# SBUF laid out by tile size: 2 KB tiles first, weight tiles 2304 bytes apart, half-width weights 64 bytes into their tile

## The chip, the core and the metric

The kernel runs on one core of a Trainium2 chip. The metric is the device time of one execution in microseconds, here as the median of three runs. SBUF is the on-chip memory of 128 partitions; an address below is a byte address within each partition.

## What is computed

The reference is two transformer blocks with two layers each, over 512 positions of width 1024, in float32. Cut to what matters here:

```python
# block 1, layer:  x += .5*rmsnorm(swiglu(rmsnorm(x)));  x += rmsnorm(token_mixer(rmsnorm(x)));  x += .5*rmsnorm(swiglu(...))
# block 2, layer:  x = layer_norm(ALPHA*x + mixer2(x));  x = layer_norm(ALPHA*x + swiglu(x))
def swiglu(h, w_gate, w_up, w_down):            # w_gate, w_up: 1024 x 2816, w_down: 2816 x 1024
    return (jax.nn.silu(h @ w_gate) * (h @ w_up)) @ w_down
proj = h @ w_in                                 # the mixers: projections, attention variants, then
return mixed @ w_out                            # an output projection
```

Nearly all the work is `activation @ weight` with weights that are read from DRAM once.

## The kernel before

**Number format.** Every float32 product runs as three products in the format float32r: a value is split in a high part and the rest, and `hi*hi + hi*lo + lo*hi` is summed in PSUM. Activations are split once and stay in SBUF: `h` (input of a projection, 16 tiles), `gu` (the gated activations of an FFN, 44 tiles) and `m` (the mixed heads, in the same 44 places), each tile 128 x 512 values, 2048 bytes in a partition.

**Weights.** `weights` loads 1024 columns of weights into a `raw` tile (3 places) by DMA on SyncE, and for each 512 columns writes a pair of `ws` tiles (14 places of 2048 bytes): ScalarE or VectorE copies the high part, VectorE or ScalarE subtracts it for the rest. A pair of `ws` tiles feeds 12 matmuls of 128 weight columns each.

**Matmuls.** `project` computes 128 output features. Its weight operand is 128 x 128 of a `ws` tile and its moving operand the activations, over all 512 positions (512 columns) or, for the first units and the last units of a stage, over one half of them (256 columns, the range `r`), so that a half can be normalised while the other is being multiplied. `vproj` computes the value projections the other way round: the `h` tile is the weight operand and a `ws` tile moves, 256 columns wide (280 for the last). Each matmul has its own weight load, and in the records the load for one matmul runs beside the matmul before it.

**Order.** A recorder collects all operations, a list scheduler with fixed costs sets the order of each engine, and `issue` emits them. A tile name has a list of places ("slots"); the scheduler gives each buffer a slot, and the pool allocates a slot's SBUF the first time that `issue` meets one of its buffers. So before the change the addresses follow the order of first use:

| operand | places | start address modulo 128 bytes |
|---|---|---|
| `ws` | 14 | all 64 |
| `h` | 16 | 64 in 12 places, 96 in 2, 0 in 2 |
| `gu`, `m` | 44 | 0 in 40 places, 64 in 4 |
| `raw` | 3 | all 64 |

A 128-column piece of a `ws` tile begins a multiple of 512 bytes into it, and the second half of an activation tile 1024 bytes into it, so these numbers hold for the operands as they are used. Below, the **phase** of a matmul is the address of the next matmul's weights (the load that runs beside it) less that of its own moving tile, modulo 128: 0 is called the same phase, 64 the opposite phase. In the program before, counting neighbouring matmuls of one shape, `h` with 256 columns has the same phase in 2542 pairs of 3386 and with 512 columns in 4446 of 5963; `gu` with 256 columns has the opposite phase in 2825 of 3111 and with 512 columns in 1432 of 1574.

## Time and profile before

| what | value |
|---|---|
| median of three runs | 3496.48 us (3493.1 to 3496.89) |
| profiled execution | 3497.46 us, span 3495.7 us |
| TensorE matmul busy | 3428.8 us, 98% of the span |
| VectorE, ScalarE busy | 2225.2 us (64%), 1738.7 us (50%) |
| granted TensorE clock, mean | 0.994 of full speed |
| bytes moved by DMA | 393.32 MB, mean 113 GB/s |

The span is the time from the first to the last instruction of the profiled execution, and 1.8 us of its own time lie around it. A recorded matmul lasts some 280 ns with 256 columns and some 397 ns with 512, but starts of neighbours are much closer than that, since they are pipelined. The quantity to look at is therefore the distance from one start to the next: the length of an unbroken row of the timeline less the last matmul's own length, divided by the count less one.

### The profile page before, as it was taken

To read this page: it belongs to the slowest core of one execution; us is meant where nothing else is said; L and a number is where in the kernel's file an instruction comes from. 1 tells how busy PE (TensorE), PEld (TensorE's weight loads), DVE (VectorE), ACT (ScalarE), POOL (GpSimd) and SP (SyncE) were. 2 spreads that over 40 slices of the span, in tenths; PEclk is the share of its full clock that TensorE was granted. 3 is DMA by queue.
4 is the path that set the end of the run, shared out by engine and by line. 5 is a ranking of instruction groups with operands and counts; after the bars stand their busy time and mean duration, and the time that the engine had idled before them with its cause. 6 is when DMAs were issued, how large, how long until landed. Compare 5 with 4: busy or idle time off the path is not lost.

```text
span 3495.7 us, 54570 instructions
## 1 busy us (share of the span) xinstructions
PE 3428.8 (98%) x20340; PEld 2964.8 (85%) x20340; DVE 2225.2 (64%) x5360; ACT 1738.7 (50%) x3681; POOL 26.8 (1%) x74
## 2 busy tenths in 40 slices
PE   8999999999999999999999999999999999999998
PEld 7887988888898889888888898879888988798888
DVE  7443898854467445998844376888333878883336
ACT  6333577643354333676533355666332656763324
POOL 0000000000000000000000000000000000000000
PEclk9999999999999999999999999999999999999999
DMA  5224532332354224522422363115223531143234
GB/s 188 97 90 139 181 103 70 127 127 96 91 163 136 94 92 139 165 65 90 137 93 95 105 194 100 50 41 173 92 97 100 188 106 61 40 141 113 93 93 135
DMA packets 121755, 393.32 MB, mean 113 GB/s; under 512 B 14829, under 2 KB 19990, under 8 KB 121489
## 3 DMA queue, kind: packets, MB, share of 16 engines
q1 hardware_dynamic: 121488, 389.83, 34.9%
q8 instruction: 160, 2.62, 0.3%
q14 instruction: 107, 0.87, 0.1%
HBM read 385.01 MB, written 4.77 MB: 112 GB/s over the span
## 4 chain that ended last, share of the span: by engine, by line
PE 84%; DVE 11%; ACT 3%; DMA 1%; issue 1%; SPq 0%; ACTq 0%; DVEq 0%
PE mm L681 76%; PE at L681 3%; DVE hw L681 2%; PE ah L681 2%; DVE ws L681 2%; PE pv L678 2%; DVE tc L681 1%; PE nb L681 1%; DVE sm L681 1%; DVE row L681 1%; DVE x L681 1%; DVE h L681 1%; DMA raw<-in_wg_dram 0%; ACT ws L681 0%; DMA cw<-in_cw_dram 0%
## 5 line engine op out<-in xcount | busy, mean ns | idle before, releaser
L681 PE MATMUL mm<-h,ws 128*128 128x512 f32 (+1 forms) x9792 | 2041.4, 358 | 13.0 <-DVE ws L681 9.7
L681 PEld LDWEIGHTS mm<-h,ws 128*128 128x128 f32 x9792 | 1623.7, 189 | 286.2 <-DVE ws L681 13.5
L681 ACT ACTIVATE ws<-raw 128x512 fp32r<-128x512 f32 (+1 forms) x1368 | 828.3, 615 | 1299.8 <-PE mm L681 1248.9
L681 DVE TENSOR_TENSOR ws<-raw,ws 128x512 fp32r<-128x512 f32 (+1 forms) x1432 | 952.6, 671 | 805.0 <-ACT ws L681 701.9
L681 PE MATMUL mm<-gu,ws 128*128 128x256 f32 (+1 forms) x4752 | 776.0, 318 | 0.0
L681 PEld LDWEIGHTS mm<-gu,ws 128*128 128x128 f32 x4752 | 674.6, 188 | 75.7 <-issue 4.4
L681 PE MATMUL mm<-ws,h 128*128 128x256 f32 (+1 forms) x1344 | 239.8, 294 | 4.3 <-ACT ws L681 1.3
L681 DVE TENSOR_TENSOR te<-te,mm 128x256 f32<-128x256 f32 (+1 forms) x228 | 99.0, 459 | 209.3 <-PE mm L681 209.3
L681 PEld LDWEIGHTS mm<-ws,h 128*128 128x128 f32 x1344 | 196.6, 190 | 9.6 <-issue 2.2
L681 PE MATMUL mm<-m,ws 128*128 128x256 f32 (+1 forms) x1248 | 203.1, 310 | 0.6 <-DVE Q L681 0.6
L681 PEld LDWEIGHTS mm<-m,ws 128*128 128x128 f32 x1248 | 167.1, 188 | 12.1 <-DVE Q L681 1.0
L681 ACT ACTIVATE row<-row,sm 128x384 f32<-128x384 f32 (+2 forms) x265 | 146.1, 564 | 39.3 <-DVE sm L681 38.1
L681 ACT ACTIVATE gu<-te 128x256 fp32r<-128x256 f32 (+1 forms) x224 | 95.4, 452 | 113.6 <-DVE te L681 113.5
L681 DVE TENSOR_TENSOR gu<-te,gu 128x256 fp32r<-128x256 f32 (+1 forms) x228 | 105.4, 464 | 14.4 <-ACT gu L681 3.0
L681 DVE TENSOR_TENSOR te<-mm,rt 128x256 f32<-128x256 f32 x176 | 67.7, 418 | 65.2 <-PE mm L681 65.2
L681 PE MATMUL at<-c_ident,row 128*128 128x128 f32 x528 | 100.5, 276 | 3.7 <-DVE row L681 1.9
L681 DVE CUSTOM_DVE_ANT_0 row<-at,T 128x128 f32<-128x128 f32 (+1 forms) x180 | 88.3, 507 | 6.3 <-PE at L681 4.9
L681 PE MATMUL ah<-hw 128*128 128x128 f32 (+1 forms) x512 | 87.8, 286 | 2.4 <-DVE hw L681 2.3
L681 ACT ACTIVATE te<-te 128x256 f32<-128x256 f32 x176 | 67.2, 417 | 45.2 <-DVE te L681 43.7
L681 ACT ACTIVATE hw<-hw 128x256 f32<-128x256 f32 (+1 forms) x176 | 74.7, 459 | 30.0 <-DVE hw L681 14.3
L681 PEld LDWEIGHTS ah<-hw 128*128 128x128 f32 x512 | 77.1, 192 | 9.4 <-DVE hw L681 2.7
L681 DVE TENSOR_TENSOR hw<-hw 128x256 f32<-128x256 f32 (+1 forms) x196 | 79.5, 422 | 5.0 <-ACT hw L681 4.3
(222 smaller groups left out, 2560.7 us busy)
## 6 DMA issues: line engine op xcount, KB each, us to landing
raw<-in_wg_dram SPq DMA_DIRECT2D x156, 512.0 KB, 3.3
raw<-in_wu_dram SPq DMA_DIRECT2D x156, 512.0 KB, 3.3
raw<-in_wd_dram SPq DMA_DIRECT2D x144, 512.0 KB, 3.5
raw<-in_wd_dram SPq DMA_DIRECT2D x72, 384.0 KB, 3.2
raw<-in_wout_dram SPq DMA_DIRECT2D x52, 512.0 KB, 3.3
raw<-in_w_f_dram SPq DMA_DIRECT2D x52, 512.0 KB, 3.3
raw<-in_win_f_dram SPq DMA_DIRECT2D x44, 512.0 KB, 3.4
raw<-in_win_v_dram SPq DMA_DIRECT2D x20, 512.0 KB, 3.6
```

Source lines behind the costliest of these rows:

```text
L678: r = nc.tensor.matmul(*args[i:i + 3], start=start and i < 6, stop=stop and i >= len(args) - 6, **kw)
L681: r = getattr(getattr(nc, op.eng), op.meth)(*args, **kw)
```

## The change

Before the first instruction is emitted, `issue` now allocates every SBUF slot in a fixed order: slots of 2048 bytes first, then `ws`, then the others from wide to narrow. A `ws` tile is declared with 576 columns (2304 bytes) instead of 512, and 512 of them are used: the first 512 where the matmuls that use the weights have 512 columns, and those from column 16 (64 bytes in) where they have 256 (`half`: `project` over half the positions, and `vproj` always).

```diff
+            first = {}
+            for op in order:
+                for b in op.bufs:
+                    if not b.dram and b.tag not in PSUM:
+                        first.setdefault(b.slot or id(b), b)
+            width = lambda b: size.get(b.slot, b.bytes())
+            for b in sorted(first.values(), key=lambda b: (width(b) != 2048, b.tag != "ws", -width(b), b.seq)):
+                real(b)
             for op in order:
                 for b in op.bufs:
                     real(b)
...
+WS_COLS = 576
...
-    def weights(self, src, n, w):
+    def weights(self, src, n, w, half):
         nc = self.nc
+        skip = 16 if half else 0
...
-            hi, lo = self.tile("ws", 512, F32R), self.tile("ws", 512, F32R)
+            hi, lo = (self.tile("ws", WS_COLS, F32R)[:, skip:skip + 512] for _ in range(2))
...
-            wt = self.weights(src[:, c * 128:(c + n) * 128], n, 128)
+            wt = self.weights(src[:, c * 128:(c + n) * 128], n, 128, r[1] - r[0] < S)
...
-            wt = self.weights(src[:, k0 * ncol:(k0 + n) * ncol], n, ncol)
+            wt = self.weights(src[:, k0 * ncol:(k0 + n) * ncol], n, ncol, True)
```

The instructions of each engine, their order and their waits are the same before and after; what differs is where the tiles lie. In the changed program every 2048-byte tile (`x`, `h`, `gu` and its sharers, `y`, `te`, `tc`) begins at 0 modulo 128, each 2048 bytes after the one before; the 14 `ws` tiles begin at 0 modulo 128, 2304 bytes apart; and weights for 256 columns begin at 64 modulo 128. By the definition above every matmul of `project` with 256 columns then has the opposite phase, every one with 512 columns the same phase, and every one of `vproj` (moving tile at 64, weights at 0) the opposite phase. The `raw` tiles begin at 0 modulo 128.

## Rows read from the trace of the kernel before

**Rows 1.** The page: busy time of each engine, granted clock by slice, chain's shares.
```profile
PE 3428.8 (98%) x20340; PEld 2964.8 (85%) x20340; DVE 2225.2 (64%) x5360; ACT 1738.7 (50%) x3681; POOL 26.8 (1%) x74
...
PEclk9999999999999999999999999999999999999999
...
PE 84%; DVE 11%; ACT 3%; DMA 1%; issue 1%; SPq 0%; ACTq 0%; DVEq 0%
PE mm L681 76%; PE at L681 3%; DVE hw L681 2%; PE ah L681 2%; DVE ws L681 2%; PE pv L678 2%; DVE tc L681 1%; PE nb L681 1%; DVE sm L681 1%; DVE row L681 1%; DVE x L681 1%; DVE h L681 1%; DMA raw<-in_wg_dram 0%; ACT ws L681 0%; DMA cw<-in_cw_dram 0%
```

**Rows 2.** Groups by shape: xcount, busy us, mean ns of one, idle before.
```profile
L681 PE MATMUL mm<-h,ws 128*128 128x512 f32 x6336 | 1585.3, 397 | 0.4 <-ACT VH L681 0.2
L681 DVE TENSOR_TENSOR ws<-raw,ws 128x512 fp32r<-128x512 f32 x1344 | 916.8, 687 | 743.8 <-ACT ws L681 669.1 <-PE mm L681 57.2 <-ACT tt L681 4.8
L681 ACT ACTIVATE ws<-raw 128x512 fp32r<-128x512 f32 x1283 | 794.6, 628 | 1205.1 <-PE mm L681 1154.6 <-DMA raw<-in_wg_dram 11.0 <-DMA raw<-in_wu_dram 6.3
L681 PE MATMUL mm<-h,ws 128*128 128x256 f32 x3456 | 474.1, 287 | 12.6 <-DVE ws L681 9.7 <-DVE te L681 1.5 <-DVE Q L681 0.7
L681 PE MATMUL mm<-gu,ws 128*128 128x256 f32 x3168 | 407.0, 280 | 0.0
L681 PE MATMUL mm<-gu,ws 128*128 128x512 f32 x1584 | 398.5, 396 | 0.0
L681 PE MATMUL mm<-ws,h 128*128 128x256 f32 x1152 | 206.3, 292 | 4.1 <-ACT ws L681 1.3 <-DVE ws L681 1.2 <-DVE sm L681 0.6
L681 PE MATMUL mm<-m,ws 128*128 128x256 f32 x960 | 131.2, 281 | 0.0
L681 PE MATMUL mm<-m,ws 128*128 128x512 f32 x288 | 93.0, 407 | 0.6 <-DVE Q L681 0.6
L681 PE MATMUL mm<-ws,h 128*128 128x280 f32 x192 | 33.5, 304 | 0.2 <-DVE NQ L681 0.2
```

**Rows 3.** Timeline of PE: start us, us, xcount; two stretches of 256 columns.
```profile
2092.57 4.09 PE L681 MATMUL mm<-h,ws 128*128 128x256 f32 x33
2086.89 3.95 PE L681 MATMUL mm<-h,ws 128*128 128x256 f32 x32
```

**Rows 4.** Timeline of PE: two other stretches of 256 columns.
```profile
1645.71 14.13 PE L681 MATMUL mm<-m,ws 128*128 128x256 f32 x123
3417.17 10.51 PE L681 MATMUL mm<-gu,ws 128*128 128x256 f32 x91
```

**Rows 5.** Timeline of PE: four stretches of 512 columns.
```profile
1877.70 4.51 PE L681 MATMUL mm<-h,ws 128*128 128x512 f32 x19
1888.77 4.54 PE L681 MATMUL mm<-h,ws 128*128 128x512 f32 x19
1911.00 4.53 PE L681 MATMUL mm<-h,ws 128*128 128x512 f32 x19
1939.83 21.78 PE L681 MATMUL mm<-gu,ws 128*128 128x512 f32 x93
```

**Rows 6.** Timeline of PE: whole stages of each kind, all phases that occur.
```profile
2790.23 15.53 PE L681 MATMUL mm<-h,ws 128*128 128x256 f32 x130
2407.51 30.69 PE L681 MATMUL mm<-h,ws 128*128 128x256 f32 x257
979.77 33.37 PE L681 MATMUL mm<-gu,ws 128*128 128x256 f32 x288
633.32 14.22 PE L681 MATMUL mm<-m,ws 128*128 128x256 f32 x122
2099.94 5.50 PE L681 MATMUL mm<-ws,h 128*128 128x256 f32 x45
2443.05 192.87 PE L681 MATMUL mm<-h,ws 128*128 128x512 f32 x835
1937.99 53.09 PE L681 MATMUL mm<-gu,ws 128*128 128x512 f32 x228
```

**Rows 7.** Windows: PE, PEld, DVE, ACT, POOL busy us, PEclk, DMA share, GB/s.
```profile
20.00:65.00 45.00, 45.00 (x364) 44.71 (x365) 40.34 (x99) 31.47 (x56) 0.00 (x0) 1.00 0.65 216
688.00:715.00 27.00, 27.00 (x228) 26.71 (x226) 25.41 (x56) 16.45 (x34) 0.00 (x0) 1.00 0.66 215
2407.00:2438.00 31.00, 31.00 (x264) 31.00 (x263) 25.68 (x56) 21.89 (x47) 0.00 (x0) 1.00 0.67 217
```

## Prediction

> **What bounds the kernel now.** I read the page first. TensorE's matmul row is busy 98% of the span, VectorE 64%, ScalarE 50%, and the chain that ended last is 84% TensorE, 76% of the span in matmuls into `mm` alone, the projections [rows 1]. The granted clock is above nine tenths in every slice, so the clock has nothing to give [rows 1]. A kernel in that state gets faster only by fewer matmuls or by a smaller distance from one matmul's start to the next. The change leaves every instruction in place, so the whole question is that distance.

> I therefore read the groups by shape for the counts [rows 2] and the timeline of TensorE for the distances, each an unbroken row's length less one matmul's own length (0.28 us with 256 columns, 0.39 us with 512), over the count less one. I chose stretches by the phase that the addresses give, with one or two odd pairs at most in each:

> - 256 columns, same phase (`h`): (4.09 - 0.28) / 32 = 119.1 ns and 3.67 / 31 = 118.4 ns [rows 3].
> - 256 columns, opposite phase (`m`, `gu`): (14.13 - 0.28) / 122 = 113.5 ns and 10.23 / 90 = 113.7 ns [rows 4].
> - 512 columns, same phase (`h`): (4.51 - 0.39) / 18 = 228.9, 230.6 and 230.0 ns, mean 229.8 [rows 5].
> - 512 columns, opposite phase (`gu`): (21.78 - 0.39) / 92 = 232.5 ns [rows 5].

> So the two widths want different things: with 256 columns the opposite phase is 5 ns shorter, with 512 columns the same phase is 2.7 ns shorter. Nothing in these rows waits for another engine. What the reader is to see is that the distance differs between equal instructions, with the address as the only known difference.

> [...]

> **The change, part by part.** Whole stages show what the mix of phases costs today [rows 6]: `h` with 256 columns (15.53 - 0.28) / 129 = 118.2 and 30.41 / 256 = 118.8, say 118.5 ns; `gu` with 256 columns 33.09 / 287 = 115.3 ns, `m` 13.94 / 121 = 115.2 ns; `vproj` 5.22 / 44 = 118.6 ns; `h` with 512 columns 192.48 / 834 = 230.8 ns; `gu` with 512 columns 52.70 / 227 = 232.2 ns. After the change all of the 256-column ones should stand at 113.6 ns and all of the 512-column ones at 229.8 ns. With the counts of [rows 2]:

> - `h`, 256 columns: 3456 x 4.9 ns = 16.9 us.
> - `gu` and `m`, 256 columns: 3168 x 1.7 + 960 x 1.6 = 6.9 us.
> - `vproj`: (1152 + 192) x 5.0 = 6.7 us.
> - `h`, 512 columns: 6336 x 1.0 = 6.3 us.
> - `gu` and `m`, 512 columns: (1584 + 288) x 2.4 = 4.5 us.

> Together 41.3 us, if every nanosecond counted. It doesn't, because part of these matmuls is not on the chain. All the `mm` matmuls at the distances above take about 2940 us (6336 x 230.8 + 1872 x 232.2 + 3456 x 118.5 + 4128 x 115.3 + 1344 x 118.6), and the chain holds 76% of 3495.7 = 2657 us of them: 0.9. I take 0.9 for the long, unbroken stages: all of 512 columns (10.8 us give 9.7) and the last units, `gu` and `m` with 256 (6.9 give 6.2).

> The first units of a stage, `h` with 256 columns, are worse off. There a pair of `ws` tiles lasts only 12 x 118.5 ns = 1.42 us, and in these stretches VectorE is busy 40.34 of 45 us, 25.41 of 27 and 25.68 of 31 [rows 7], 90, 94 and 83%; the first of them already runs at 45 us / 364 = 123.6 ns, above the 118.5 of an unhindered row, and the group has its idle time behind `ws` of VectorE, 9.7 us [rows 2]. If TensorE gets 4% faster, VectorE's 94% becomes 98%: it still fits, but hardly, and any wait for `ws` that TensorE now meets a little earlier takes the gain back. Nothing gained is one end, 0.9 the other; I take 0.6, nearer the upper end because the tile that limits (687 ns of VectorE in 1.42 us [rows 2]) leaves room: 10.2 us. DMA moves 216 GB/s there [rows 7] and would have to move 4% more; the group has no idle time from a DMA, so I cost it at nothing, and if it does not follow, the same 10.2 us are lost.

> For `vproj` the trace has almost no steady stretch in the opposite phase with the `ws` tile moving, so the price is bounded by 118.6 ns (nothing) and 113.6 ns (all). These matmuls sit between attention heads, with waits around them. I take 0.4: 2.7 us.

> What the change adds costs nothing that a row shows. A `ws` tile is 256 bytes longer, but the same 512 columns are written and read. The writers of `ws` and the readers of `raw` start at other addresses; the copy and the subtraction occur before at one phase only, so a loss there is not excluded. At 687 ns each and 1344 of them, 2% longer would add 18 us to VectorE, which is idle for 36% of the span and would show it only in the start stages, some 4 us. I take 0. A gain there would be as small.

> Sum: 9.7 + 6.2 + 10.2 + 2.7 = 28.8 us. The profiled execution took 3497.46 us in its own time (span 3495.7 and 1.8 around it), so the changed one should take 3468.7; the median of the runs is 1.0 us lower, which gives **3468 us**, 0.8% faster.

> **The rivals.**

> - **Only the 256-column part works.** The changed 512-column matmuls all read at 0 modulo 128 with weights at 0; the same phase before was 64 with 64. If the absolute address counts too, they could stand at the 232.5 ns of `gu` [rows 5]: 6336 x 1.7 x 0.9 = 9.7 us lost instead of 9.7 gained, and 3468 + 19 = 3487 us. For it: the three stretches of the same phase scatter from 228.9 to 230.6. Against: each of them lies below every opposite one. The same time, about 3490, results if the start stages and `vproj` give nothing because VectorE sets their pace.
> - **Slower.** With 512 columns all weights and all moving tiles now begin at one phase, for stretches of hundreds of matmuls instead of 18. If then each weight load costs what it costs in the same phase with 256 columns, 4.9 ns, the 8208 matmuls lose 8208 x 4.9 x 0.9 = 36 us against 19 gained: 3496.5 + 17 = 3514 us. The point from which this decides is a distance with 512 columns of about 231.1 + 19 / (8208 x 0.9) = 234 ns. Against it: no same-phase row comes near it.
> - **The change does nothing.** If `h` is slow for a reason other than its phase, such as its place in the start stages beside a busy VectorE, distances stay and the time is 3496 us within 0.2%. [...] For it: the slow and the fast rows of 256 columns do come from different stages. Against: `m` and `gu` at 113.6 ns come from stages with weight conversions at the same pace, 12 matmuls to a pair, and `h` with 512 columns, in a calm stage, is the faster one.

> **How the numbers follow.** The forecast has 0.59, the first rival with its variant 0.19, no effect 0.14, slower 0.08. About 0.2% (7 us) is what a measurement of this kernel can tell from no change; 3487 and 3490 lie 0.27% and 0.19% below the median, so a little of the first rival goes to "same". That gives faster 0.76, same 0.16, slower 0.08. The range: below, the 512 columns at their best row (228.9, another 0.9 x 8208 x 0.9 = 6.6 us), `h` at 0.9 (5.1 us) and `vproj` at 0.9 (3.3 us) give 3453, and with a distance a little under any seen 3446; above, the first rival's 3487 to 3490. The forecast's own range is 3453 to 3480.

> **What would show it.** In the changed kernel's timeline: rows of `h` with 256 columns at 113 to 115 ns instead of 118.5; `gu` with 256 columns near 113.6 throughout, without the rise at its four odd tiles; `h` and `gu` with 512 columns both at 229 to 231; `vproj` at 114 or still 118.6. In the windows of the start stages, VectorE's share should rise by some 4% of itself, and the waits of `mm` for `ws` on VectorE may grow from 9.7 us. The copy into `ws` on ScalarE should stay at 628 ns and the subtraction on VectorE at 687 [rows 2]. The prediction is wrong if 512 columns stand above 231, or if `h` with 256 columns stays at 118 while its addresses are in the opposite phase.

## Result and the profile after

The changed kernel takes 3456.68 us (median, 3453.73 to 3457.36) against 3495.95 us for the kernel before in the same comparison: a ratio of 0.9887, 95% interval 0.987 to 0.9905, or 39 us less. The forecast was 3468 us, 28 less. Its profiled execution took 3457.36 us in its own time with a span of 3455.6 us.

The page of the changed kernel, busy time of each engine, answers to [rows 1]:

```profile
PE 3386.9 (98%) x20340; PEld 2952.9 (85%) x20340; DVE 2222.5 (64%) x5360; ACT 1739.2 (50%) x3681; POOL 26.9 (1%) x74
...
PE 82%; DVE 12%; ACT 3%; issue 1%; DMA 1%; SPq 0%; ACTq 0%; DVEq 0%
```

TensorE's busy time falls by 41.9 us, the other engines' stays. The groups by shape of the changed kernel (count, busy us, mean ns of one, idle before) answer to [rows 2]:

```profile
L689 PE MATMUL mm<-h,ws 128*128 128x512 f32 x6336 | 1561.6, 393 | 0.5 <-DVE D L689 0.2 <-ACT VH L689 0.2
L689 DVE TENSOR_TENSOR ws<-raw,ws 128x512 fp32r<-128x512 f32 x1344 | 916.4, 687 | 721.5 <-ACT ws L689 654.5 <-PE mm L689 50.0 <-ACT tt L689 4.7
L689 ACT ACTIVATE ws<-raw 128x512 fp32r<-128x512 f32 x1283 | 794.7, 628 | 1166.7 <-PE mm L689 1111.1 <-DMA raw<-in_wg_dram 9.3 <-DMA raw<-in_wu_dram 5.8
L689 PE MATMUL mm<-h,ws 128*128 128x256 f32 x3456 | 466.8, 285 | 13.2 <-DVE ws L689 10.3 <-DVE Q L689 0.7 <-DVE h L689 0.6
L689 PE MATMUL mm<-gu,ws 128*128 128x256 f32 x3168 | 406.2, 280 | 0.0
L689 PE MATMUL mm<-gu,ws 128*128 128x512 f32 x1584 | 390.5, 391 | 0.0
L689 PE MATMUL mm<-ws,h 128*128 128x256 f32 x1152 | 204.6, 289 | 4.4 <-DVE K L689 2.2 <-DVE ws L689 1.2 <-DVE sm L689 0.6
L689 PE MATMUL mm<-m,ws 128*128 128x256 f32 x960 | 129.9, 280 | 0.0
L689 PE MATMUL mm<-m,ws 128*128 128x512 f32 x288 | 92.5, 405 | 0.6 <-DVE Q L689 0.6
...
L689 PE MATMUL mm<-ws,h 128*128 128x280 f32 x192 | 33.2, 302 | 0.2 <-DVE NQ L689 0.2
```

Group by group against [rows 2], in busy time: 512 columns lose 23.7 + 8.0 + 0.5 = 32.2 us, 256 columns only 7.3 (`h`) + 0.8 (`gu`) + 1.3 (`m`) + 1.7 (`vproj`) = 11.1 us, and the last 280 columns of `vproj` 0.3 us. The copy and the subtraction into `ws` keep their 628 and 687 ns. So the gain is real and of the forecast's kind, but it sits where the forecast had the smaller part of it.

The timeline of TensorE says why: start us, length us, count. Distances are worked out as before.

```profile
739.62 150.67 PE L689 MATMUL mm<-h,ws 128*128 128x512 f32 x664
1934.69 25.55 PE L689 MATMUL mm<-gu,ws 128*128 128x512 f32 x112
...
29.82 34.44 PE L689 MATMUL mm<-h,ws 128*128 128x256 f32 x291
2384.77 27.48 PE L689 MATMUL mm<-h,ws 128*128 128x256 f32 x241
970.79 13.47 PE L689 MATMUL mm<-gu,ws 128*128 128x256 f32 x113
986.82 13.42 PE L689 MATMUL mm<-gu,ws 128*128 128x256 f32 x117
498.28 4.64 PE L689 MATMUL mm<-ws,h 128*128 128x256 f32 x38
```

With 512 columns the distance is (150.67 - 0.39) / 663 = 226.7 ns for `h` and 25.16 / 111 = 226.7 ns for `gu`, for hundreds of matmuls on end, where [rows 6] had 230.8 and 232.2 and the best short stretch of [rows 5] 228.9. With 256 columns these rows show two values: 34.16 / 290 = 117.8 and 27.20 / 240 = 113.3 ns for `h`, 117.8 and 113.3 ns for two neighbouring stretches of `gu`, 117.8 ns for `vproj`. All of these have the opposite phase.

### The profile page after: what moved, and what is told of

It reads as the page before. It is cut to its first block, busy times and chain, and to the rows that moved or that the text cites. A ratio compares the mean times of both kernels' runs of the same rounds, so it can differ in the third digit from the quotient of the medians.

```text
span 3455.6 us, 54570 instructions
## 1 busy us (share of the span) xinstructions
PE 3386.9 (98%) x20340; PEld 2952.9 (85%) x20340; DVE 2222.5 (64%) x5360; ACT 1739.2 (50%) x3681; POOL 26.9 (1%) x74
## 4 chain that ended last, share of the span: by engine, by line
PE 82%; DVE 12%; ACT 3%; issue 1%; DMA 1%; SPq 0%; ACTq 0%; DVEq 0%
PE mm L689 75%; PE at L689 3%; DVE hw L689 2%; DVE ws L689 2%; PE ah L689 2%; PE pv L686 1%; DVE tc L689 1%; DVE row L689 1%; PE nb L689 1%; DVE sm L689 1%; DVE x L689 1%; DVE D L689 1%; ACT ws L689 1%; DMA raw<-in_wg_dram 1%; DVE h L689 0%
## 5 line engine op out<-in xcount | busy, mean ns | idle before, releaser
L689 PE MATMUL mm<-h,ws 128*128 128x512 f32 (+1 forms) x9792 | 2010.3, 355 | 13.7 <-DVE ws L689 10.3
L689 PE MATMUL mm<-gu,ws 128*128 128x256 f32 (+1 forms) x4752 | 767.4, 317 | 0.0
L689 PEld LDWEIGHTS mm<-ws,h 128*128 128x128 f32 x1344 | 194.8, 188 | 10.2 <-issue 4.1
L689 ACT ACTIVATE gu<-te 128x256 fp32r<-128x256 f32 (+1 forms) x224 | 95.3, 452 | 114.7 <-DVE te L689 114.6
L689 ACT ACTIVATE hw<-hw 128x256 f32<-128x256 f32 (+1 forms) x176 | 74.8, 459 | 27.5 <-DVE hw L689 14.9
```

Of the source, the lines that this page charges most:

```text
L689: r = getattr(getattr(nc, op.eng), op.meth)(*args, **kw)
```

## Experiments

Three readings were to be told apart: **P**, the phase of weights and moving tile modulo 128 decides; **U**, a uniform start of all tiles is enough; **S**, the spacing of the weight tiles does it. Each edit is against the changed kernel.

**e1_no_shift**: no weights shifted.

```diff
-        skip = 16 if half else 0
+        skip = 0
```

> The changed kernel with no weights shifted by 64 bytes: every matmul, with 256 columns too, has the same phase. Theory P (the phase modulo 128 decides the distance): 512 columns stay at 226.9 ns, 256 columns go to some 118.4 ns from 115.6 (h), 114.7 (gu) and 114.0 (m), so 3456 x 2.8 x 0.6 + 3168 x 3.7 x 0.9 + 960 x 4.4 x 0.9 = 20 us more than the changed kernel: 3477 us. Theory U (it is enough that all tiles begin at one residue, whatever the phase): 256 columns stay near 115, 3457 us.

**e2_all_shift**: all weights shifted, for 512 columns too.

```diff
-        skip = 16 if half else 0
+        skip = 16
```

> The changed kernel with all weights shifted by 64 bytes, so that matmuls with 512 columns have the opposite phase too. Theory P: 512 columns go from 226.9 to the 232.5 ns of gu before the change, 8208 x 5.6 x 0.9 = 41 us: 3498 us; 256 columns as in the changed kernel. Theory U: nothing changes, 3457 us.

**e4_ws_2048**: as e1_no_shift, and weight tiles 2048 bytes apart.

```diff
-WS_COLS = 576
+WS_COLS = 512
...
-        skip = 16 if half else 0
+        skip = 0
```

> As e1_no_shift, and the 14 weight tiles 2048 instead of 2304 bytes apart, so that all of them begin at one address modulo 2048. Theory P: the spacing does nothing, the time of e1_no_shift (3477 us by P) within 0.2%. Theory S (the spacing of the weight tiles is what brought 512 columns from 230 to 226.9): 512 columns at 230 ns, 8208 x 3.1 x 0.9 = 23 us above e1_no_shift.

**e5_old_order**: the shift and the 2304-byte tiles with the old order of addresses.

```diff
-            for b in sorted(first.values(), key=lambda b: (width(b) != 2048, b.tag != "ws", -width(b), b.seq)):
-                real(b)
```

> Only the 2304-byte weight tiles and the 64-byte shift, with the addresses given out in the order of first use as before: h lies at 64, 96 and 0 modulo 128 and gu mostly at 0; weights for 512 columns begin at 64, those for 256 at 0, so that gu and m with 256 columns lose the opposite phase and most of h gets it. Theory P: h with 256 columns gains part of 4.9 ns, 5 to 8 us, gu and m go from 115.2 to 118.4 ns, 4128 x 3.2 x 0.9 = 12 us, 512 columns stay at 230.8 and 232.2: 3500 us. Theory U: no uniform residue, so 3496 us as before. If the shift alone were what helps: below 3490.

| run | us | ratio to before, 95% interval | distance, 512 columns | distance, 256 columns |
|---|---|---|---|---|
| e1_no_shift | 3482.49 | 0.9961, 0.9949 to 0.9974 | same phase, 226.7 ns | same phase, 120.0 ns |
| e2_all_shift | 3511.29 | 1.0043, 1.003 to 1.0057 | opposite phase, 233.3 ns | opposite phase, 113.3 ns |
| e4_ws_2048 | 3481.36 | 0.996, 0.9947 to 0.9974 | same phase, 226.7 ns | same phase |
| e5_old_order | 3510.82 | 1.004, 1.0026 to 1.0054 | as before: 1586.2 (`h`) and 398.3 us (`gu`) busy | `gu` same phase, 119.4 ns |

Timeline of TensorE in e1_no_shift, a stretch of `gu` with 256 columns, 10.20 / 85 = 120.0 ns:

```profile
3399.78 10.48 PE L689 MATMUL mm<-gu,ws 128*128 128x256 f32 x86
```

Timeline of TensorE in e2_all_shift, the stage of `h` with 512 columns, 150.27 / 644 = 233.3 ns, and the group with its busy time:

```profile
739.61 150.66 PE L689 MATMUL mm<-h,ws 128*128 128x512 f32 x645
```
```profile
L689 PE MATMUL mm<-h,ws 128*128 128x512 f32 x6336 | 1597.8, 399 | 0.4 <-DVE D L689 0.2
```

In the same 150 us this stage gets 645 matmuls instead of 664. Two other groups of e2_all_shift:

```profile
L689 PE MATMUL mm<-gu,ws 128*128 128x256 f32 x3168 | 409.9, 281 | 0.0
L689 PE MATMUL mm<-gu,ws 128*128 128x512 f32 x1584 | 400.6, 397 | 0.0
```

U falls with both runs: the tiles are as uniform as in the changed kernel, and 64 bytes less on the weights for 256 columns cost 25.8 us (3482.49 against 3456.68), 64 bytes more on those for 512 columns 54.6 us. Of the 54.6 us, the groups with 512 columns hold 36.2 (`h`) + 10.1 (`gu`) + 0.4 (`m`) = 46.7 us of busy time, which is 0.86 of 8208 x (233.3 - 226.7) = 54 us; `gu` and `m` with 256 columns, whose addresses did not change, hold another 3.7 + 2.5 us (why they can differ is shown with e12 below). That the writers of `ws`, whose addresses move too, disturb TensorE does not fit: in e2's stage from 740 to 890 us VectorE is busy 72.78 of 150 us and ScalarE 52.58, while all 642 distances between starts there are 230, 231, 235 or 236 ns. S falls with e4_ws_2048: without the shift, 2304 or 2048 bytes make no difference (3482.49 and 3481.36 us), and its group of `h` with 512 columns is as fast as the changed kernel's:

```profile
L689 PE MATMUL mm<-h,ws 128*128 128x512 f32 x6336 | 1561.9, 393 | 0.3 <-ACT VH L689 0.2
```

e5_old_order is the control the other way round. Groups with 256 columns in it:

```profile
L687 PE MATMUL mm<-h,ws 128*128 128x256 f32 x3456 | 472.9, 287 | 14.1 <-DVE ws L687 9.8 <-DVE te L687 2.5 <-DVE Q L687 0.7
L687 PE MATMUL mm<-gu,ws 128*128 128x256 f32 x3168 | 418.3, 284 | 0.0
...
L687 PE MATMUL mm<-m,ws 128*128 128x256 f32 x960 | 135.4, 286 | 0.0
```

`gu` and `m` have lost their opposite phase and 11.3 and 4.2 us with it, at their old addresses; `h`, which mostly gained it but keeps three kinds of address in its tiles, is better by 1.2 us only. The shift without the new order makes the kernel slower than before, by 14.9 us.

P is right in kind in all four runs, but its amounts were too small: 20 us above the changed kernel expected for e1_no_shift and 25.8 measured, because 256 columns went to 120.0 ns and not to 118.4; 41 and 54.6 for e2_all_shift; 3500 us and 3510.82 for e5_old_order, where `h` gained 1.2 us and not 5 to 8. The distances behind them, 118.4 and 232.5 ns, had been read from the mixed addresses of the old layout.

**e3_pad_first**: everything 64 bytes further on, all phases kept.

```diff
+            pools["sb"] = self.ctx.enter_context(tc.tile_pool(name="sbuf", bufs=1))
+            pools["sb"].tile([128, 16], F32, name="pad", tag="pad")
             for b in sorted(first.values(), key=lambda b: (width(b) != 2048, b.tag != "ws", -width(b), b.seq)):
```

> The changed kernel with a 64-byte tile allocated before all others, so that every tile begins at 64 instead of 0 modulo 128; all phases (weights less moving tile) stay. Theory P (only the difference counts): 512 columns at 226.9 ns, 256 columns at 114 to 115.6, 3457 us within 0.2%. Theory A (an absolute start at a multiple of 128 bytes is what helps): 512 columns at 230 ns, 256 columns at 118, 8208 x 3.1 x 0.9 + some 15 = 38 us more: 3495 us.

3456.94 us, ratio 0.9891 (0.9877 to 0.9906), and the timeline of TensorE in it has 226.7 and 113.3 ns:

```profile
739.82 150.44 PE L691 MATMUL mm<-h,ws 128*128 128x512 f32 x663
...
2399.79 12.40 PE L691 MATMUL mm<-h,ws 128*128 128x256 f32 x108
```

Moving both addresses by 64 bytes changes nothing (3456.94 against 3456.68 us): here it is their difference that counts, and an absolute start at a multiple of 128 bytes is not what helps.

**e7_shift_32b, e10_shift_96b, e9_shift_128b**: `skip = 8`, `24` and `32` for 256 columns in place of 16.

```diff
-        skip = 16 if half else 0
+        skip = 8 if half else 0
```

> Weights for 256 columns shifted by 32 bytes instead of 64. Theory P with a phase that works by degrees: halfway between no shift (119.9 ns, 3482 us) and 64 bytes (113.3 or 117.8 ns, 3457 us), some 117 ns and 3469 us. Theory H (whole 64-byte halves of 128 bytes count, and a load that starts inside one meets both): as bad as no shift, 119 to 120 ns, 3482 us.

> Weights for 256 columns shifted by 96 bytes instead of 64. By degrees it should be like 32 bytes, some 117 ns and 3469 us, if only the distance to the nearest multiple of 128 counts; if it matters which of the two streams is ahead, 32 and 96 bytes differ, and one of them may hold the 113.3 ns row throughout: 256 columns at 113.5 everywhere would give 3 to 8 us less than the changed kernel, 3450 us.

> Weights for 256 columns shifted by 128 bytes instead of 64. Theory P (the phase counts modulo 128): as no shift, 119.9 ns with 256 columns and 3482 us. If the phase counts modulo 256 or more: between 113.3 and 119.9 ns, and 3457 to 3475 us.

They took 3475.03 us (ratio 0.9939, 0.9925 to 0.9954), 3473.58 us (0.9936, 0.9921 to 0.9951) and 3484.22 us (0.996, 0.9948 to 0.9973). Timelines of TensorE, one stretch of `h` with 256 columns each, in this order, 118.3, 117.3 and 120.1 ns:

```profile
2399.80 12.47 PE L689 MATMUL mm<-h,ws 128*128 128x256 f32 x104
```
```profile
2399.82 12.36 PE L689 MATMUL mm<-h,ws 128*128 128x256 f32 x104
```
```profile
2399.77 12.41 PE L689 MATMUL mm<-h,ws 128*128 128x256 f32 x102
```

With 256 columns 128 bytes give the time of no shift (3484.22 and 3482.49 us), so in the total 0 and 128 count as one phase; that 64 and 192 do not is shown below. No run shifts the weights for 512 columns by anything but 0 and 64 bytes. 32 and 96 bytes, at 3475.03 and 3473.58 us, lie between no shift, 3482 us, and the halfway value, 3469 us; neither reading of e7 fits well.

**e12_changed_again, e11_vproj_192b, e8_shift_192b**: why two values with 256 columns? In `project` the weights lie 64 bytes ahead of the moving tile modulo 256, in `vproj` 64 behind.

e12_changed_again has no edit. e11_vproj_192b:

```diff
-        skip = 16 if half else 0
+        skip = 16 * int(half)
...
-            wt = self.weights(src[:, k0 * ncol:(k0 + n) * ncol], n, ncol, True)
+            wt = self.weights(src[:, k0 * ncol:(k0 + n) * ncol], n, ncol, 3)
```

e8_shift_192b:

```diff
-        skip = 16 if half else 0
+        skip = 48 if half else 0
```

> The changed kernel once more, on the chip of the two runs beside it, for a fine comparison: 3457 us, and again two kinds of rows with 256 columns, near 113.3 and near 117.8 ns, maybe not in the same stages as in its first profile (three and more of the stages with 256 columns change their kind if the kind is settled by chance).

> The changed kernel with vproj's weights, which move there, shifted by 192 bytes instead of 64, so that the weight operand lies 64 bytes ahead modulo 256 as in project, and not 64 behind. Theory D (of the two opposite phases, 64 ahead lets the row settle at 113.3 ns and 64 behind at 117.8): vproj goes from 117.6 to 114 ns, 1344 x 3.6 x 0.4 to 0.9 = 2 to 4 us less. Theory P alone (modulo 128): no change, 117.6 ns, the time of e12_changed_again.

> All weights for 256 columns shifted by 192 bytes: project's lie 64 bytes behind modulo 256, vproj's operands 64 ahead. Theory D: h, gu and m with 256 columns settle at 117.8 ns throughout, 3456 x 2.5 x 0.6 + 4128 x 3.2 x 0.9 = 17 us above the changed kernel, less 2 to 4 for vproj: 3471 us. Theory P alone: as the changed kernel, 3457 us.

They took 3459.07 us (ratio 0.9896, 0.9882 to 0.9909), 3458.43 us (0.9892, 0.9878 to 0.9905) and 3467.56 us (0.9917, 0.9904 to 0.9931). e12's timeline has the first stage of `h`, which ran at 117.8 ns in the changed kernel's first profile from end to end, in both values, 8.25 / 70 = 117.9 and 12.58 / 111 = 113.3 ns:

```profile
29.74 8.53 PE L689 MATMUL mm<-h,ws 128*128 128x256 f32 x71
...
51.32 12.86 PE L689 MATMUL mm<-h,ws 128*128 128x256 f32 x112
```

The program is the same one, so the value is not settled by the addresses alone but in the execution (whether both ran on the same chip is not known), and it is kept until the row is broken: in the changed kernel the two halves of each of the 73 stretches counted next, past its first eight matmuls, agree within 1.5 ns. I counted, in each trace, the unbroken stretches of 30 or more matmuls with 256 columns by their mean distance past the first eight: in the changed kernel 42 of 73 lie below 114 ns, 28 above 117; in e12 46 and 28 of 77; in e8 9 and 61 of 72; in e1 none and 68 of 68. Of stretches of `project` alone, 41 of 61 lie below 114 ns in the changed kernel and 4 of 61 in e8; of `vproj` alone, none of 4 in the changed kernel and 3 of 4 in e11. So the lean of theory D shows in both: 64 behind settles at the longer value nearly always, 64 ahead more often at the shorter. The time of e8 is 8.5 us above e12, where theory D had 13 to 15 and P alone none, and e8's fastest run, 3464.14, lies above e12's slowest, 3460.14. So with 256 columns the phase does not count modulo 128 alone: 64 and 192 bytes differ. The timelines of `vproj` in e11 (4.09 / 36 = 113.6 ns) and of `h` in e8 (12.25 / 104 = 117.8 ns):

```profile
1498.29 4.37 PE L689 MATMUL mm<-ws,h 128*128 128x256 f32 x37
```
```profile
2399.72 12.53 PE L689 MATMUL mm<-h,ws 128*128 128x256 f32 x105
```

`vproj` does reach the shorter value in e11, but the time, 3458.43 us, lies inside e12's 3457.69 to 3460.14. From the distances 1152 x (117.8 - 113.6) ns = 4.8 us is the most that I estimate for it, and only 4 of the stretches counted are of `vproj` alone. No version that is measurably faster than the changed kernel came out of this.

## Why the prediction was right, and where its sizes were off

- **Phase as the cause.** Right. e1, e2 and e3 show it with nothing else changed: 64 bytes move the rows of 512 columns from 226.7 to 233.3 ns. The rival "does nothing" falls with that.
- **512 columns: 9.7 us in the sum, 32.2 us of busy time measured.** This is the term that was mis-sized: the distance aimed at was 229.8 ns and is 226.7. The three stretches of [rows 5] were the same phase modulo 128 but not modulo 256, because the old `h` and `ws` tiles began at 64 in some places and at 192 in others, modulo 256. Put beside the addresses, 37 of their 54 distances lie at 0 modulo 256 with a mean of 228.1 ns, 14 at 128 with 233.1, and 3 at 64 with 234.7. In the changed kernel all lie at 0 modulo 256. That the mixture makes the difference is read from these rows; no run holds 512 columns at 128 throughout. The factor of 0.9 was right: 0.9 x (6336 x 4.1 + 1872 x 5.5) = 32.6 us with 226.7 ns.
- **The first units, `h` with 256 columns: 10.2 us in the sum, 7.3 measured.** Near, but for another reason, which is luck. VectorE did not eat the gain: the waits of `mm` for `ws` grew only from 9.7 [rows 2] to 10.3 us, and VectorE's share did not rise by 4% of itself, not even in the late stage that did gain (25.56 us in place of 25.68 [rows 7]). Nor was the first window a sign of it: its 123.6 ns on average come from the first six microseconds, 33 matmuls at 182 ns, and the other 39 us have 333 at 117 ns (first fence below). What halved the gain is that the row settles at 117.8 ns in part of the stretches. That is the forecast's own sign of being wrong, `h` at 118 in the opposite phase, and it came for these stretches.
- **The last units, `gu` and `m` with 256 columns: 6.2 us in the sum, 0.8 + 1.3 measured.** Of [rows 4] I had taken two stretches that had settled at 113.5; others with the same phase settle at 117.8, as 970.79 us shows. The forecast that `gu` would stand "near 113.6 throughout" was wrong.
- **`vproj`: 2.7 us in the sum, 1.7 + 0.3 measured**, at 117.8 ns, its opposite phase being the one 64 behind.
- **No cost from longer tiles or moved writers.** Right: 628 and 687 ns, as before.
- **The sum.** 39 us measured against 28 is as near as it is because, in busy time, 512 columns gave 22.5 us more than their terms and the rest nearly 8 less: two errors that partly cancel, which is luck.
- **The rivals.** "Only the 256-column part works" went the other way: the 512-column part works best. Its reason, an absolute address that counts, falls with e3. "Slower" named e2's loss with the sign of the phase reversed; there the kernel was slower than before at 233.3 ns already, below the 234 ns worked out, because 256 columns gained much less than the 19 us of the sum.

Windows for the third point (busy us of PE, PEld, DVE, ACT, POOL, clock, DMA share, GB/s), first of the kernel before, its first start stage in two parts:

```profile
20.00:26.00 6.00, 6.00 (x33) 5.71 (x34) 5.90 (x13) 3.68 (x8) 0.00 (x0) 1.00 0.67 214
26.00:65.00 39.00, 39.00 (x333) 39.00 (x332) 34.44 (x88) 27.79 (x48) 0.00 (x0) 1.00 0.64 216
```

Then of the changed kernel's start stages:

```profile
20.00:65.00 45.00, 44.77 (x362) 44.51 (x363) 40.63 (x100) 31.64 (x56) 0.00 (x0) 1.00 0.64 216
...
2384.00:2415.00 31.00, 31.00 (x271) 30.79 (x270) 25.56 (x57) 22.91 (x49) 0.00 (x0) 1.00 0.67 221
```

The late stage, settled at 113.3 ns, does 271 matmuls in 31 us where [rows 7] had 264; the first, settled at 117.8 ns, does 362 in 45 us where it had 364.

## What to carry to other kernels

Where TensorE is busy all the time, here 98% of the span, and nothing else can be cut, the distance between matmul starts is a quantity to tune, and the address of the weights against that of the moving operand is one of its settings, here worth 226.7 against 233.3 ns with 512 columns and 113.3 against 120.0 ns with 256: try 0 and 64 bytes for each width of the moving operand, and 64 both ahead and behind, with all tiles of a kind at one residue modulo 256, and read the distance off long rows of the timeline. The runs show this for float32r matmuls of 256 and 512 columns with a weight load each, and for nothing else. A price read from a program of mixed addresses understated what a uniform one gives (118.4 and 232.5 ns read, 120.0 and 233.3 measured). And the shift without the layout that goes with it made the kernel 14.9 us slower (e5).
